# Eight 1 MB weight loads near the end of a two-layer trunk, each issued as five row pieces

## The chip, the cores and the metric

The kernel runs on one core of a Trainium2 chip. The metric is device time in microseconds (us), the median of several executions; lower is better. Names of engines are those of the profile: PE is TensorE, PEld its weight loads, DVE is VectorE, ACT is ScalarE, POOL is GpSimd and SP is SyncE, whose sequencer issues the weight loads. A DMA that SP issues is carried out by the core's 16 DMA engines.

## What is computed

Two layers of a hybrid encoder trunk over 256 tokens of width 1024. Each layer runs three branches (differential attention, a causal pooling mixer, attention to 256 memory tokens), gates and merges them, and then a channel mixer. In the second layer, where the change lies, the mixer is a top-2-of-8 expert SwiGLU:

```python
def moe_swiglu(h, w_router, w1, w3, w2):
    ...
    comb = jnp.einsum('tk,tke->te', gates, jax.nn.one_hot(idx, N_EXPERTS, dtype=h.dtype))
    out = jnp.zeros_like(ht)
    for e in range(N_EXPERTS):
        out = out + comb[:, e:e + 1] * swiglu(ht, w1[e], w3[e], w2[e])
    return out.reshape(B, S, D)
```

w1 and w3 of an expert are 1024 x 3584, w2 is 3584 x 1024, all float32.

## The kernel before

All weights lie in one DRAM tensor `w` of blocks of 128 rows x 2048 float32 (1 MB, 8 KB a row), laid out on the host in the order in which they are used. Half a block (128 x 1024) is a unit. The class `Stream` walks through the units: `load` (L190) takes a free 1 MB buffer, issues one block into it from SP (L201) and goes on as long as a buffer is free; `give` (L226) puts a buffer back after its last use and calls `load` again. The very first block and the very last one are cut into three column pieces (`ends`); all others are one DMA of 128 partitions x 8 KB.

The order of the blocks is fixed by `plan`. After the dense layer the expert stage goes through eight places of seven steps each; place 0 is expert 0, and the other experts are ranked at run time by their token counts, so that the block's address is a register on SP (`src`, `at`). A place has a fixed number of token rows, `ROWS = (96, 64, 96, 64, 96, 64, 96, 64)`. A step has an up part, `up` (L1179: four blocks, matmuls of 32 token columns against 256 weight columns in four array tiles), and a down part, `down` (L1205: two blocks), one step behind. So a place takes 42 blocks, and the last place, of 64 rows, takes the last 42 blocks of the run. After the last matmul the result is evacuated (L1224, L1226), scattered back to the tokens (L1128, L1133) and stored (`finish`, L853).

In the expert stage some eighteen buffers of 1 MB rotate: four of the ring, four that held split pairs before, and those of tiles that the attention no longer needs (`W.widen` calls). Matmuls here read the loaded float32 block directly, without a step in between (`raw`).

The framework gives every DMA one of a fixed set of semaphores, in turn; a DMA that takes a semaphore waits on SP until the DMA that had it before has landed. SP runs its program in order, so everything behind a waiting DMA waits too. A reader of a buffer waits for all DMAs that wrote it.

Of the kernel before, what the change touches and what calls it, by code (L numbers as in the profile page):

```python
# [32 lines left out]
ROWS = (96, 64, 96, 64, 96, 64, 96, 64)  # L33
LARGEST = [p for p in range(1, NE) if ROWS[p] == max(ROWS)]
RANKS = [0 if p == 0 else 1 + (LARGEST + [q for q in range(1, NE) if q not in LARGEST]).index(p) for p in range(NE)]
LANES = np.arange(512).reshape(4, 4, 32)


# [9 lines left out]
def plan():  # L48
# [21 lines left out]
    def lanes(e, parts):  # L70

        per = 512 // sum(len(p) for p in parts)
        units.extend([(t, e, np.arange(r + q, r + q + 128), p) for q in range(0, per * 128, 128)
                      for p in parts for t in ("moe_w1", "moe_w3")] for r in range(0, D, per * 128))
# [21 lines left out]
    for e in range(NE):  # L96
        for c in range(FE // 512):
            where["up", c] = len(units) // 2 - first - e * EXPERT
            if e == 0 and c == 0:
                lanes(e, [LANES[:, :2].transpose(1, 0, 2).ravel()])  # L100
                lanes(e, [LANES[j, 2:].ravel() for j in range(4)])
            else:
                lanes(e, [c * 512 + LANES[j].ravel() for j in range(4)])
            where["down", c] = len(units) // 2 - first - e * EXPERT
            units.extend([("moe_w2", e, c * 512 + LANES[:, q].ravel(), np.arange(D))] for q in range(4))
    order = [(0, k - first) for k in range(first)]
# [47 lines left out]
class Stream:  # L154
# [39 lines left out]
    def load(self, most=99):  # L194
        while self.loaded < self.total and self.free and most:
            slot = self.free.popleft()
            u, n = self.loaded, 2
            raw = slot[0]()
            ends = {0: (0, 512, 1024, 2048), self.total - 2: (0, 1024, 1536, 2048)}.get(u, (0, 2048))
            for c, e in zip(ends, ends[1:]):  # L200
                self.nc.sync.dma_start(raw[:, c:e], self.src(u, c, e - c))  # L201
            for i in range(n):
                self.raws[u + i] = (raw[:, i * 1024:(i + 1) * 1024], slot if i == n - 1 else None)
            self.loaded += n
            most -= 1
# [40 lines left out]
def trunk(ctx: ExitStack, tc: tile.TileContext, a, out, stage=99):  # L246
# [685 lines left out]
    for p in range(NE):  # L932
        nc.gpsimd.memset(ranks[:, p:p + 1], float(RANKS[p]))
        nc.gpsimd.memset(rows[:, p:p + 1], float(ROWS[p]))
# [449 lines left out]
```

## Time and profile before

| | before |
|---|---|
| median of 3 runs | 1632.04 us (1631.81 to 1632.33) |
| profiled execution | 1631.46 us, span 1629.7 us |
| PE busy | 1581.9 us, 97% |
| DVE / ACT busy | 645.4 us / 521.6 us |
| DMA moved | 493.78 MB, 303 GB/s over the span |
| 1 MB weight loads on SP | 455, median 19.8 us from issue to landing |

The span is the time from the first to the last instruction of one profiled execution; the device time of the same execution is a little longer. The page cuts the span into 40 slices of 40.7 us and gives the busy share of each engine and of the DMA engines in tenths. Below it stands the chain that ended last, and what each engine waited for. A busy PE is not a PE at its peak: matmul ends are modelled.

### The profile page before, as it was taken

The page shows a single profiled execution, that of the slowest core. Times are in us where ns is not written, and L with a number is a line of the kernel's source. Part 1 is how long each engine was busy: PE and PEld are TensorE (multiplying, and loading weights), DVE is VectorE, ACT ScalarE, POOL GpSimd, SP SyncE. Part 2 cuts the span into 40 slices and gives each one's busy share as a digit, 9 for nine tenths or more (in the row PEclk, how much of TensorE's full clock was granted, in tenths as well). Part 3 has the DMA queues.
Part 4 walks back from the last instruction along what each step waited for, and adds up shares of the span by engine and source line. Part 5 has one row for each costly group of instructions (what it writes and reads, how often), then busy time and mean ns, then how long its engine had stood idle before and what let it go on. Part 6 is the DMA issues. An engine that isn't in the chain of part 4 may idle for free.

```text
span 1629.7 us, 39421 instructions
## 1 busy us (share of the span) xinstructions
PE 1581.9 (97%) x17511; PEld 1110.2 (68%) x17511; DVE 645.4 (40%) x1261; ACT 521.6 (32%) x877; POOL 7.8 (0%) x36
## 2 busy tenths in 40 slices
PE   9999999999999999999999999999999998899987
PEld 6888788788888887787866555665556654466553
DVE  6676876655656666776410212112021120110201
ACT  7676654544545666554300101001000010000100
POOL 0000000000000000000000000000000000000000
PEclk9999999999999999999999999999999999999999
DMA  9544365454554434667889999999999999999996
GB/s 381 205 150 159 142 220 182 171 180 180 189 190 162 188 134 161 235 224 280 340 329 393 418 417 418 417 417 418 418 418 418 418 418 418 417 410 417 412 410 245
DMA packets 69809, 493.78 MB, mean 303 GB/s; under 512 B 7904, under 2 KB 8160, under 8 KB 10752
## 3 DMA queue, kind: packets, MB, share of 16 engines
q1 hardware_dynamic: 67824, 485.68, 75.4%
q0 software_dynamic: 1232, 4.82, 0.9%
q8 instruction: 139, 2.28, 0.6%
q10 hardware_dynamic: 576, 0.69, 0.1%
q14 instruction: 38, 0.31, 0.1%
HBM read 490.11 MB, written 1.05 MB: 301 GB/s over the span
## 4 chain that ended last, share of the span: by engine, by line
PE 76%; DMA 20%; DVE 1%; ACT 1%; issue 0%; SPq 0%; ACTq 0%
PE acc L392 41%; DMA raw<-in_w_dram 20%; PE acc L1179 18%; PE y L1205 9%; PE xgp L1042 1%; PE sc L1128 1%; PE ds L643 1%; PE tT L504 1%; PE do L683 1%; DMA E<-in_x_t_dram 0%; PE mo L587 0%; PE ms L554 0%; DVE pair L219 0%; DVE yf L1224 0%; ACT yf L1226 0%
## 5 line engine op out<-in xcount | busy, mean ns | idle before, releaser
L1179 PE MATMUL acc<-raw,xg 128*32 128x256 f32 (+1 forms) x8960 | 508.2, 378 | 19.6 <-DMA raw<-in_w_dram 17.9
L1179 PEld LDWEIGHTS acc<-raw,xg 128*32 128x32 f32 x8960 | 290.3, 110 | 216.8 <-issue 25.8
L219 DVE TENSOR_TENSOR pair<-raw,pair 128x1024 fp32r<-128x1024 f32 (+1 forms) x247 | 300.4, 1219 | 222.6 <-ACT pair L218 221.9
L392 PE MATMUL acc<-pair,bigB 128*128 128x512 f32 x1536 | 375.4, 399 | 2.2 <-ACT pair L218 1.7
L218 ACT ACTIVATE pair<-raw 128x1024 fp32r<-128x1024 f32 (+1 forms) x247 | 260.1, 1055 | 289.4 <-PE acc L392 275.7
L392 PEld LDWEIGHTS acc<-pair,bigB 128*128 128x128 f32 x1536 | 284.1, 188 | 72.0 <-ACT pair L218 2.6
L1205 PE MATMUL y<-raw,gt 128*32 128x256 f32 x4480 | 255.4, 379 | 9.0 <-DMA raw<-in_w_dram 8.0
L1190 DVE TENSOR_TENSOR junk<-acc,junk 128x256 f32<-128x256 f32 (+2 forms) x83 | 29.2, 377 | 562.0 <-ACT junk L1189 562.0
L1189 ACT ACTIVATE junk<-acc 128x256 f32<-128x256 f32 (+2 forms) x83 | 28.9, 348 | 664.4 <-PE acc L1179 663.1
L392 PE MATMUL acc<-pair,bigA 128*128 128x512 f32 (+1 forms) x960 | 219.8, 386 | 0.7 <-ACT g L822 0.4
L1205 PEld LDWEIGHTS y<-raw,gt 128*32 128x32 f32 x4480 | 147.5, 110 | 106.9 <-DMA raw<-in_w_dram 7.9
L392 PEld LDWEIGHTS acc<-pair,bigA 128*128 128x128 f32 x960 | 172.4, 188 | 38.9 <-ACT g L822 0.8
L392 PE MATMUL acc<-pair,E 128*128 128x512 f32 x456 | 108.8, 396 | 0.0
L392 PEld LDWEIGHTS acc<-pair,E 128*128 128x128 f32 x456 | 84.7, 188 | 20.9 <-issue 1.3
L1192 DVE STREAM_TRANSPOSE gt<-junk 128x128 f32<-128x128 f32 (+1 forms) x140 | 33.2, 283 | 1.0
L654 ACT ACTIVATE dp<-dp,dmn 128x128 f32<-128x128 f32 (+1 forms) x64 | 28.5, 446 | 10.1 <-DVE dmn L650 9.8
L1128 PE MATMUL sc<-ys,GT 96*128 96x512 f32 (+1 forms) x56 | 22.3, 477 | 9.1 <-ACT ys L366 8.3
L1133 DVE SCALAR_TENSOR_TENSOR total<-sc,misc,total 128x512 f32<-128x512 f32 x28 | 20.8, 750 | 24.8 <-PE sc L1128 24.6
L1226 ACT ACTIVATE yf<-y 32x256 f32<-32x256 f32 x48 | 18.0, 375 | 37.6 <-PE y L1205 37.1
L1042 PEld LDWEIGHTS xgp<-xg,x 128*128 128x128 f32 x160 | 20.8, 190 | 6.7 <-issue 6.6
L1224 DVE COPY yf<-y 32x256 f32<-32x256 f32 x32 | 13.4, 420 | 29.2 <-PE y L1205 28.9
L1049 ACT ACTIVATE xg<-xgp,cols 128x160 f32<-128x160 f32 (+2 forms) x20 | 6.0, 365 | 58.9 <-PE xgp L1042 58.9
(245 smaller groups left out, 783.5 us busy)
## 6 DMA issues: line engine op xcount, KB each, us to landing
raw<-in_w_dram SPq DMA_DIRECT2D x455, 1024.0 KB, 19.8
bb<-in_b_gate_dram POOLq DMA_DIRECT2D x6, 512.0 KB, 4.5
E<-in_mem_t_dram SPq DMA_DIRECT2D x2, 1024.0 KB, 10.8
raw<-in_w_dram SPq DMA_DIRECT2D x4, 256.0 KB, 10.0
raw<-in_w_dram SPq DMA_DIRECT2D x2, 512.0 KB, 12.6
x<-in_x_dram SPq DMA_DIRECT2D x1, 1024.0 KB, 13.5
E<-in_mem_dram SPq DMA_DIRECT2D x1, 1024.0 KB, 19.8
bias<-in_bias_dram POOLq DMA_DIRECT2D x1, 1024.0 KB, 8.0
```

Of the source, the lines that this page charges most:

```text
L218: nc.scalar.activation(t[:, 0, sl], src[:, sl], AF.Copy)
L219: nc.vector.tensor_tensor(t[:, 1, sl], src[:, sl], t[:, 0, sl].bitcast(F32), OP.subtract)
L392: nc.tensor.matmul(accs(tb, b)[:, :n], s, w[:, off:off + n], start=begin and (tb, b) not in started, stop=end and n_ == 2 and last[b] == ( ...
L654: nc.scalar.activation(p[:, 1, m, :kl], p[:, 0, m, :kl], AF.Exp, scale=-1.0, bias=mn[:, m:m + 1], accum_out=s0[:, b, h + i:h + i + 1] if m ...
L1042: nc.tensor.matmul(t[:, i], x[:, tb, (k0 + i) * 128:(k0 + i + 1) * 128], G[tuple(es)][:, tb], start=tb == 0, stop=tb == 1)
L1128: nc.tensor.matmul(t, gt[:, tb], ys[p][:, j * 512:(j + 1) * 512], start=p == 0, stop=p == len(ys) - 1)
L1133: nc.vector.scalar_tensor_tensor(xo, t, comb[:, tb, e:e + 1], x[:, tb, sl] if e == 0 else xo, op0=OP.mult, op1=OP.add)
L1179: nc.tensor.matmul(t[32 * j:32 * j + 32, c0:c0 + n], XG[e][:, k, 32 * r:32 * r + 32], w[:, (4 * m + j) * n:(4 * m + j + 1) * n], start=k = ...
L1189: nc.scalar.activation(g[:, r0:r1], v[:, :, 0], AF.Silu)
L1190: nc.vector.tensor_tensor(g[:, r0:r1], v[:, :, 1], g[:, r0:r1], OP.mult)
L1192: nc.vector.transpose(gts[i][:, r, 4 - width // 32:].rearrange("p q t -> p (q t)"), g[:, r])
L1205: nc.tensor.matmul(t[32 * j:32 * j + 32, c0:c0 + 256], gt[:, r, q], w[:, 256 * j:256 * j + 256], start=first and q == 0 and r < 2, stop=la ...
```

## The change

`load` issues eight of the blocks, those 24 to 17 from the end, as five DMAs instead of one: rows 0 to 95, then rows 96 to 103, 104 to 111, 112 to 119 and 120 to 127, each of 8 KB a row. The bytes, the buffer and the readers are the same.

```diff
+LEAN = range(-24, -16)
...
             ends = {0: (0, 512, 1024, 2048), self.total - 2: (0, 1024, 1536, 2048)}.get(u, (0, 2048))
+            cuts = [0, 128]
+            if u // 2 - self.total // 2 in LEAN:
+                cuts = [0, 96, 104, 112, 120, 128]
             for c, e in zip(ends, ends[1:]):
-                self.nc.sync.dma_start(raw[:, c:e], self.src(u, c, e - c))
+                src = self.src(u, c, e - c)
+                for p, q in zip(cuts, cuts[1:]):
+                    self.nc.sync.dma_start(raw[p:q, c:e], src[p:q])
```

## Rows read from the trace of the kernel before

**Rows 1.** The page: busy tenths of PE and DMA, and GB/s, in 40 slices.

```profile
PE   9999999999999999999999999999999998899987
...
DMA  9544365454554434667889999999999999999996
GB/s 381 205 150 159 142 220 182 171 180 180 189 190 162 188 134 161 235 224 280 340 329 393 418 417 418 417 417 418 418 418 418 418 418 418 417 410 417 412 410 245
```

**Rows 2.** Chain that ended last, 1480 to 1632 us: start us, us, what.

```profile
1488.01 4.87 PE acc L1179 x89
1492.88 21.24 DMA raw<-in_w_dram
...
1514.24 19.88 DMA raw<-in_w_dram
...
1615.44 3.69 PE y L1205 x64
```

**Rows 3.** What SP's queue waited for, 1490 to 1630 us: us in total, times, longest.

```profile
SPq L201 <- DMA raw<-in_w_dram: 89.6, 45, 2.8
...
SPq L201 <- PE acc L1179: 1.0, 3, 0.4
SPq L201 <- PE y L1205: 0.8, 2, 0.4
```

**Rows 4.** Timeline of SP, two stretches: start us, us, instruction, count.

```profile
1539.18 64.00 SPq L201 DMA_DIRECT2D raw<-in_w_dram  x26
...
1557.13 0.33 SPq L201 DMA_DIRECT2D raw<-in_w_dram  x1
```

**Rows 5.** Line L201, 1480 to 1630 us: ns min/median/max of each instruction; landing.

```profile
L201 SPq MOVE raw<-in_w_dram x49: 29/29/29, 1480.4 to 1600.8; - x49
L201 SPq DMA_DIRECT2D raw<-in_w_dram x49: 332/333/338, 1480.4 to 1602.8; - x49
L201 SPq FUSED_REGOPS  x48: 55/55/75, 1480.8 to 1600.7; - x48
L201 SPq EVENT_SEMAPHORE  x47: 17/17/17, 1480.3 to 1597.9; - x47
...
DMA to landing us min/median/max: 15.1/20.1/21.3
```

**Rows 6.** The DMA view, 1300 to 1500 us: packets of all sizes; SP's queue with packets, MB, share.

```profile
DMA packets 11405, 83.26 MB, mean 416 GB/s; under 512 B 1267, under 2 KB 1267, under 8 KB 1267
...
q1 hardware_dynamic: 11376, 82.82, 100.4%
```

**Rows 7.** Windows of 2 us at the end; the last two columns are DMA share, GB/s.

```profile
1602.00:1604.00 2.00, 1.54 (x32) 0.70 (x28) 0.00 (x0) 0.00 (x0) 0.00 (x0) 1.00 0.86 340
1604.00:1606.00 2.00, 1.43 (x28) 0.65 (x24) 0.00 (x0) 0.00 (x0) 0.00 (x0) 1.00 0.68 266
1606.00:1608.00 2.00, 1.44 (x30) 0.66 (x24) 0.00 (x0) 0.00 (x0) 0.00 (x0) 1.00 0.53 209
1608.00:1610.00 2.00, 1.80 (x32) 0.80 (x27) 0.00 (x0) 0.14 (x1) 0.00 (x0) 1.00 0.48 201
1610.00:1612.00 2.00, 1.55 (x31) 1.13 (x32) 0.93 (x3) 0.25 (x1) 0.00 (x0) 1.00 0.51 213
1612.00:1614.00 2.00, 1.53 (x32) 0.73 (x28) 0.00 (x0) 0.00 (x0) 0.00 (x0) 1.00 0.50 209
1614.00:1616.00 2.00, 1.34 (x28) 0.68 (x24) 0.00 (x0) 0.00 (x0) 0.00 (x0) 1.00 0.48 189
1616.00:1618.00 2.00, 2.00 (x44) 1.48 (x39) 0.00 (x0) 0.00 (x0) 0.00 (x0) 1.00 0.26 89
```

**Rows 8.** Chain that ended last, in an earlier place of 64 rows.

```profile
1335.68 6.91 PE acc L1179 x128
```

**Rows 9.** DMA issues of the whole run: KB each, median us to landing.

```profile
out_dram<-total SPq DMA_DIRECT2D x2, 256.0 KB, 2.9
...
E<-in_x_t_dram SPq DMA_DIRECT2D x1, 128.0 KB, 3.2
```

## The prediction, made before the changed kernel ran

> **What bounds the kernel.** I began with the page's slices [rows 1]. From the 23rd slice on the DMA rate is flat at about 417 GB/s with a busy share of 9 tenths or more, while PE's own digits fall in the last slices: the expert stage streams weights at a ceiling. Then the chain of waits [rows 2]: PE is on it until 1493 us, and from there to 1615 us, where PE takes over again, it is almost nothing but weight loads, one hanging on another, each some 20 us long; PE adds its last 3.7 us and the scatter. In a place of 64 rows PE needs 6.91 us for four blocks, 1.73 us a block [rows 8]; a block arrives every 2.5 us. So in the last place the time is set by when the last block has landed, and the changed loads lie in the middle of that stretch: the 26 issues from 1539.2 us on [rows 4] are 23 whole blocks and the three pieces of the last, so the first of them is the block 24 from the end, and the one 17 from the end goes out at 1557.1 us. A microsecond lost or won by the loads there reaches the end unless it is made up later, and nothing in the last 60 us has room to make it up.
>
> Next, how the loads are paced. One block takes 1048576 bytes / 418 GB/s = 2.51 us [rows 1]; it lands 20.1 us after its issue [rows 5]. 20.1 / 2.51 = 8: eight DMAs are outstanding, always. The chain shows the same: a load is issued 0.12 us after an earlier one landed (1492.88 + 21.24 = 1514.12, the next at 1514.24) [rows 2]. And SP waited 45 times in this stretch for a weight DMA and five times, 1.8 us in all, for a buffer [rows 3]. So the limit is eight DMAs in flight, counted in DMAs and not in bytes.
>
> Last, the end of the stream [rows 7]. The busy share does not drop from 1 to 0: it falls between 1602 and 1606 us to 0.5, stays there with 200 to 213 GB/s, and goes to 0 after 1617 us. Half of the 16 engines had finished, and the other half still worked at the same rate each (209 / 8 = 26.1 GB/s, as 418 / 16). The share missing from 1602 to 1616 us is 2.96 windows of 2 us, 5.9 us of all engines or 11.8 us of eight. So one half of the engines, the leading half, runs 11.8 us ahead of the other, the lagging half. Which numbers they have no view shows.
>
> **The change, step by step.** *Rows per engine.* 82.82 MB are 79 blocks, and they go with 11376 packets, 144 a block; 1267 packets, 16 a block, are under 512 B [rows 6]. So 128 remain: one packet per row of 8 KB. At 26.1 GB/s a row takes 0.314 us. The piece of 96 rows gives each engine 6 rows. A piece of 8 rows is 8 packets, so it cannot be on more than eight engines; I take it that the four pieces of a block go to the same eight. These carry 6 + 4 = 10 rows a block (3.13 us), the other eight 6 (1.88 us), where all carried 8 (2.51 us). Over eight blocks that is 16 rows, 5.0 us, moved from one half to the other.
>
> [...]
>
> *SP's queue.* Five DMAs a block cost SP 5 x (0.333 + 0.029 + 0.055 + 0.017 us) = 2.2 us [rows 5], below 3.13 us, so the issuing itself is hidden by the transfers. What isn't hidden is the limit of eight. From 1539.2 to 1557.1 us eight old blocks land on the lagging half, and each landing lets SP issue one DMA. Before, that was eight blocks; now it is 96, 8, 8, 8, 8, 96, 8 and 8 rows, not two blocks. If the pieces go to the leading half, it had 20.1 - 11.8 = 8.3 us of old work and gets 6 + 4 + 6 + 2 = 18 rows, 5.6 us: it runs dry and its lead is spent on waiting. The lagging half ends its old work at 1557.0 us and then has two pieces of 6 rows.
>
> *From there on.* Still to be moved by the eight engines: 2 rows of the second block and six blocks of 10, 62 rows. The first of them waits for the first large piece, which lands on the lagging half at 1557.0 + 1.9 = 1558.9 us. From issue to landing without data I take 2.6 us: a store of 256 KB takes 2.9 us, less 0.6 of data, and a load of 128 KB 3.2 us, less 0.3 [rows 9]. So the first row lands at 1559.0 + 2.6 + 0.3 = 1561.9 us, the other 61 follow in 19.1 us, and 0.3 us go between the first few, whose issues come singly: 1581.3 us. Sixteen whole blocks at 2.51 us follow on the same engines: 1621.5 us. The same count for the kernel before is 1557.0 + 24 x 2.51 = 1617.2 us, and its transfers do stop there [rows 7]. Difference: +4.3 us. With the fixed part at 2.3 or 2.9 us it is +4.0 or +4.6; if the restart cost nothing, +1.7.
>
> If the eight are the lagging half, nothing runs dry: the half that ends last carries 16 rows more, +5.0 us. I sum with +4.3: the two differ by less than the uncertainty.
>
> *What costs nothing.* 32 more DMAs with their small packets: 8 rows alone are 2.51 us and so is a block, so a small packet is under 0.01 us. Matmuls that read a split block wait for five semaphores: at SP's 17 ns a wait that is 0.6 us for all eight blocks, covered by PE's 0.78 us of slack in every block; uncovered, it would be those 0.6 us. Buffers: eighteen stand against eight loads in flight, and the waits for them are 1.8 us [rows 3].
>
> Sum: 1631.46 us (the profiled execution) + 4.3 = 1635.8; the median stands 0.58 us above that execution: **1636.3 us**.
>
> **Rivals.** *The rows shift and nothing runs dry: faster.* Half the engines stand idle for the last 11.8 us. If the pieces go to the leading half and SP gets them out without the wait for the eighth DMA back, so that the leading half always has rows, it ends 5.0 us later and the lagging half 5.0 us earlier, with 1.8 us of lag left: 1632.04 - 5.0 = 1627.0 us. For it: the 0.5 share [rows 7], and that 5.0 us is near half of 11.8. Against it: the 45 waits [rows 3]. It decides if the leading half's queue outlasts the 18 us from 1539 us on; by the rows it holds 13.9 us of work.
>
> *Rows that share a way into the buffer: slower still.* [...] If neighbours share a path, a row takes longer: between 0.31 us (no sharing) and 2.51 us (all eight share one). With a threefold time, near the middle on a doubling scale, four pieces cost 4 x 0.63 = 2.5 us more a block; over the 6.2 blocks of the 62 rows that is 15.6 us: 1652 us. Twofold it is +7.8 (1644), fourfold +23 (1660). Nothing in this trace is so narrow, so nothing speaks for or against it.
>
> [...]
>
> *The pieces don't lean on one half.* If successive pieces go to different eights in turn, every engine still carries 8 rows a block, the lag stays, and the end moves by less than the restart cost: 1632 to 1634 us. That a piece is at most eight packets leaves open which eight engines take them.
>
> **Chances.** Forecast (same eight, no sharing) 0.40; sharing 0.27; faster 0.17; no lean 0.16. A measurement of this kernel can tell about 0.2%, 3.3 us, from no change. The forecast's low end, +1.7, lies under that, so I give 0.08 of its 0.40 to "same". Slower by over 0.2%: 0.32 + 0.27 = 0.59; within: 0.16 + 0.08 = 0.24; faster: 0.17. The range takes in the forecast's bounds, the no-lean case, the half of the faster case that falls short of its full gain, and sharing up to about threefold: 1629 to 1654 us; what it leaves out (full gain 0.09, more sharing 0.08) is under 0.2.
>
> **What would show it.** In the profile after, 447 loads of 1024 KB, 8 of 768 KB and 32 of 64 KB; packets under 512 B are 32 x 8 = 256 more than before if each small piece uses eight engines, and twice that if it uses sixteen. Windows of 2 us: from about 1547 to 1560 us the DMA share falls towards 0.5 to 0.7, then stays near 0.8 (16 engines carry 128 rows in the time of 10 on eight) until about 1581 us; the last 12 us no longer stand at 0.5 if the leading half was the one loaded, and stand there longer if the other was. SP's waits for a weight DMA rise from 45 to about 75. With sharing, the middle stretch has a share near 1 (packets take longer) at 200 to 300 GB/s and lasts over 30 us. The forecast is wrong if the rate stays near 418 GB/s through 1540 to 1580 us, or if the end comes before 1630 us.

## The result, and the profile after

The changed kernel takes 1655.12 us (1654.03 to 1656.54) against 1631.92 in the same comparison: a ratio of 1.0143, 95% interval 1.0131 to 1.0155. It is 23 us slower. The forecast was slower by 4.3 us, with a range that ends at 1654.

The page of the changed kernel, first the DMA slices and then packets, SP's queue and SP's larger pieces:

```profile
span 1652.3 us, 39533 instructions
...
DMA  9544455455554544658989999999999999999897
GB/s 380 202 146 158 152 202 186 176 181 181 192 185 167 178 145 159 258 203 313 350 336 397 418 417 418 417 417 418 418 418 417 418 418 419 417 411 413 263 281 306
DMA packets 70067, 493.79 MB, mean 299 GB/s; under 512 B 8161, under 2 KB 8417, under 8 KB 11009
...
q1 hardware_dynamic: 68080, 485.69, 75.5%
...
raw<-in_w_dram SPq DMA_DIRECT2D x447, 1024.0 KB
raw<-in_w_dram SPq DMA_DIRECT2D x8, 768.0 KB
```

The stream is as before up to the 37th slice [rows 1 have 417, 412, 410 and 245 in the last four]; then two slices fall to 263 and 281 GB/s. SP's queue has 68080 packets. The page of the kernel before has 67824:

```profile
q1 hardware_dynamic: 67824, 485.68, 75.4%
```

So 256 came with the 32 small pieces: eight each, where a whole block has 16. That fits eight engines a piece, half of those at work on whole blocks (a share of 1.01), and loads of eight neighbouring rows by themselves kept a share of 0.50, eight of 16, in the second run of dead loads below.

What the stretch looks like, in windows of 10 us and as a whole (the last two columns are DMA share and GB/s):

```profile
1540.00:1550.00 10.00, 10.00 (x165) 5.45 (x168) 2.85 (x6) 0.38 (x1) 0.00 (x0) 1.00 0.88 250
1550.00:1560.00 10.00, 9.25 (x175) 5.27 (x167) 0.93 (x3) 0.38 (x1) 0.00 (x0) 1.00 0.66 201
1560.00:1570.00 10.00, 5.54 (x96) 3.01 (x88) 0.00 (x0) 0.00 (x0) 0.00 (x0) 1.00 0.63 166
...
1590.00:1600.00 10.00, 5.94 (x64) 3.80 (x64) 0.00 (x0) 0.00 (x0) 0.00 (x0) 0.66 0.89 243
...
1540.00:1600.00 60.00, 41.52 (x613) 22.78 (x612) 4.71 (x12) 1.15 (x3) 0.00 (x0) 0.89 0.80 219
```

The same 60 us of the kernel before:

```profile
1540.00:1600.00 60.00, 53.36 (x906) 29.30 (x902) 6.57 (x18) 1.92 (x5) 0.00 (x0) 0.99 1.01 413
```

This closes the account. In these 60 us 219 GB/s move 13.14 MB, which at 418 GB/s would take 31.4 us; 28.6 us are lost. The share says in which way. At 0.80 the engines stood idle for 20% of the time, 12.0 us. While they were busy they were slow: a row of 8 KB took on average 0.80 x 16 x 8192 B / 219 GB/s = 0.48 us of one engine, where whole blocks had shown 0.314, and that is the other 16.6 us. Two things are set against the 28.6: 0.7 us that the kernel before loses in the same window (413 instead of 418), and the tail. Windows of 2 us at the end of the changed kernel:

```profile
1636.00:1638.00 2.00, 1.47 (x28) 0.64 (x20) 0.00 (x0) 0.00 (x0) 0.00 (x0) 1.00 0.99 389
1638.00:1640.00 2.00, 1.87 (x36) 1.43 (x40) 0.00 (x0) 0.00 (x0) 0.00 (x0) 1.00 0.39 143
```

Where the kernel before worked its last 12 us with half its engines [rows 7], all sixteen now end within a microsecond or two. The 5.9 us that half the engines had stood idle are won back. 28.6 - 0.7 - 5.9 = 22.0 us, and the spans differ by 22.6.

The chain of waits shows that not only the new pieces are slow:

```profile
1516.88 20.37 DMA raw<-in_w_dram
...
1537.36 26.53 DMA raw<-in_w_dram
...
1618.19 19.81 DMA raw<-in_w_dram
```

The block issued at 1537.36 us is a whole one, the last before the split ones. It took 26.5 us to land, with cut blocks beside it, against about 20 for whole blocks before and after the stretch.

### The profile page after: what moved, and what is told of

Read it like the earlier page. It is cut to its first block, busy times and chain, and to the rows that moved or that the text cites. A ratio compares the mean times of both kernels' runs of the same rounds, so it can differ in the third digit from the quotient of the medians.

```text
span 1652.3 us, 39533 instructions
## 1 busy us (share of the span) xinstructions
PE 1589.7 (96%) x17511; PEld 1111.7 (67%) x17511; DVE 645.5 (39%) x1261; ACT 521.7 (32%) x877; POOL 7.9 (0%) x36
## 3 DMA queue, kind: packets, MB, share of 16 engines
q1 hardware_dynamic: 68080, 485.69, 75.5%
q8 instruction: 139, 2.28, 0.6%
## 4 chain that ended last, share of the span: by engine, by line
PE 77%; DMA 20%; DVE 1%; ACT 1%; issue 0%; SPq 0%; ACTq 0%
PE acc L398 41%; DMA raw<-in_w_dram 19%; PE acc L1185 19%; PE y L1211 9%; PE xgp L1048 1%; PE sc L1134 1%; PE ds L649 1%; PE tT L510 1%; PE do L689 1%; DMA E<-in_x_t_dram 0%; PE mo L593 0%; PE ms L560 0%; DVE pair L225 0%; DVE yf L1230 0%; PE xT L445 0%
## 5 line engine op out<-in xcount | busy, mean ns | idle before, releaser
L1134 PEld LDWEIGHTS sc<-ys,GT 96*128 96x128 f32 (+1 forms) x56 | 9.5, 200 | 22.7 <-ACT ys L372 11.5
```

Of the source, the lines that this page charges most:

```text
L1134: nc.tensor.matmul(t, gt[:, tb], ys[p][:, j * 512:(j + 1) * 512], start=p == 0, stop=p == len(ys) - 1)
```

## The experiments

Three theories stood: the small pieces' neighbouring rows slow each other (A); the queue of eight DMAs and the uneven rows alone cost the 23 us (B); every DMA over a part of the rows is slow, the 96-row piece too (C). Four kernels came first.

**The small pieces take every fourth row.**

```diff
-                for p, q in zip(cuts, cuts[1:]):
-                    self.nc.sync.dma_start(raw[p:q, c:e], src[p:q])
+                rows = [slice(p, q) for p, q in zip(cuts, cuts[1:])]
+                if len(cuts) > 2:
+                    rows = [slice(0, 96)] + [slice(96 + j, 128, 4) for j in range(4)]
+                for r in rows:
+                    self.nc.sync.dma_start(raw[r, c:e], src[r])
```

> Same eight blocks, same count of DMAs and same rows per engine as the changed kernel, but each 8-row piece takes every fourth row of rows 96 to 127 instead of eight neighbours. Theory A (the small pieces' neighbouring rows slow each other): the time falls to the sum without sharing, about 1632 + 4 = 1636 us. Theory B (the queue of eight DMAs and the uneven rows alone cost the 23 us): no change, 1655 us. Theory C (the 96-row piece is slowed too, on all engines): it stays over 1645 us.

Measured: 1650.9 us, ratio 1.0115 (1.0098 to 1.0132), 4 us less than the change. SP's issues in this kernel (min/median/max in ns, then a stretch of the timeline), and below them those of the changed kernel:

```profile
L210 SPq DMA_DIRECT2D raw<-in_w_dram x51: 326/644/825, 1535.7 to 1602.7; - x51
...
1565.70 28.05 SPq L210 DMA_DIRECT2D raw<-in_w_dram  x33
...
L207 SPq DMA_DIRECT2D raw<-in_w_dram x81: 277/332/364, 1481.1 to 1625.5; - x81
```

The 4 us are not the price of the neighbourhood. A piece of every fourth row takes SP about 0.64 us to issue, where one of eight neighbours takes 0.28, and SP gets out 33 DMAs in 28.05 us, 0.85 us each or 4.25 us a block. Five issues one right behind the other take 4.07 us (1566.61 to 1570.68), so nearly all of that is SP's own time. At that pace the stretch is slow whatever its rows cost, and this run cannot tell what the neighbourhood is worth. Theory A falls with the next run.

**Two pieces, 96 and 32 rows.** No small pieces and no uneven engines: SP's queue has 67952 packets, 128 more than before, 16 for each piece of 32 rows.

```diff
-                cuts = [0, 96, 104, 112, 120, 128]
+                cuts = [0, 96, 128]
```

> The eight blocks in two DMAs, of 96 and 32 neighbouring rows; if 32 rows spread over all 16 engines, each engine carries 8 rows a block as before. Theory C (a piece of fewer than 128 rows is slow because its rows collide): +10 to +17 us, 1642 to 1649. Theory A (only the 8-row pieces) and B: 0 to +1 us, 1632 to 1633.

Measured: 1654.98 us, ratio 1.0143 (1.0127 to 1.0160), the same as the change itself. Cutting a block once between two rows costs as much as the whole change, so A alone is out. The window of this kernel, and one of its tail:

```profile
1540.00:1600.00 60.00, 41.73 (x630) 23.77 (x625) 4.71 (x12) 1.15 (x3) 0.00 (x0) 0.91 0.95 239
...
1634.00:1636.00 2.00, 1.54 (x32) 0.80 (x28) 0.11 (x1) 0.00 (x0) 0.00 (x0) 1.00 0.52 214
```

Here the engines are hardly idle (0.95) and a row takes 0.95 x 16 x 8192 / 239 GB/s = 0.52 us. The tail at half share is still there. So the two kernels come to the same time by different sums: the change idles 9 us more and has rows that are a little faster, and it wins the tail back.

**Five pieces by columns.** The same sizes and count, each over all 128 rows.

```diff
-                cuts = [0, 96, 104, 112, 120, 128]
+                ends = (0, 1536, 1664, 1792, 1920, 2048)
```

> The same eight blocks in five DMAs of the same sizes (768 KB and four times 64 KB), but cut by columns, each over all 128 rows: same count in the queue of eight, no uneven engines, no neighbours. Theory A and C (sharing): 0 to +3 us, 1632 to 1635. Theory B (the count in the queue): most of the 23 us stays, over 1645 us.

Measured: 1640.13 us, ratio 1.0052 (1.0036 to 1.0069): 8 us slower, between the two expectations. SP's timeline in the middle of it:

```profile
1559.70 23.46 SPq L207 DMA_DIRECT2D raw<-in_w_dram  x33
```

SP gets out 33 pieces in 23.46 us, 0.71 us each, so a block of five takes 3.6 us and not 2.51. I had put SP's own time at 2.2 us a block; one right behind the other the pieces go out 0.54 to 0.60 us apart, 2.8 us a block. The stretch as a whole, and the end of the stream:

```profile
1540.00:1590.00 50.00, 40.14 (x676) 22.54 (x672) 5.25 (x15) 1.54 (x4) 0.00 (x0) 1.00 0.84 296
...
1622.00:1624.00 2.00, 1.33 (x28) 0.59 (x21) 0.00 (x0) 0.00 (x0) 0.00 (x0) 1.00 0.99 383
1624.00:1626.00 2.00, 2.00 (x44) 1.47 (x40) 0.00 (x0) 0.00 (x0) 0.00 (x0) 1.00 0.23 80
```

At 296 GB/s the 50 us lose 14.6. Of these 8.0 are idle engines (0.84), and 6.6 are busy ones that are slower with the narrow pieces among their work: on average 0.84 x 16 x 8192 / 296 = 0.37 us for 8 KB. The tail at half share is gone here too, although a piece does not lean on few engines: SP's queue has 72432 packets, 4608 more than before, 144 for each of the 32 added pieces, as many as a whole block has. 14.6 - 0.7 - 5.9 = 8.0 us, and the spans differ by 8.2.

**Two odd blocks.** An attempt to lean on few engines with two DMAs instead of five.

```diff
-LEAN = range(-24, -16)
+LEAN = (-24, -20)
...
-                cuts = [0, 96, 104, 112, 120, 128]
+                cuts = [0, 119, 128]
```

> Leans on few engines with two DMAs instead of five: only blocks 24 and 20 from the end, cut in 119 and 9 rows. If 119 rows go on seven engines (17 rows each) and 9 on nine, the leading half takes about 20 rows more (6.3 us) and the lagging half 14 to 16 rows less (4.4 us). Without slow rows in the piece: 1632 - 4.5 = 1627.5 us. If its neighbouring rows slow each other about as in the changed kernel (a row in 0.55 instead of 0.31 us): 34 rows take 18.7 us, beyond the leading half's lead, and the time is 1632 to 1641 us.

Measured: 1653.64 us, ratio 1.0133 (1.0116 to 1.0150). Two cut blocks cost 22 us, more than either expectation. SP's queue has 67824 packets, as before, so the two pieces of a block have 16 small packets together; that agrees with seven engines and nine, if each adds one, and no view shows which engines they are. SP's timeline from 1539 to 1545 us:

```profile
1539.13 2.66 SPq L207 DMA_DIRECT2D raw<-in_w_dram  x2
```

A window right after, and one near the end:

```profile
1545.00:1550.00 5.00, 5.00 (x99) 2.99 (x92) 0.78 (x3) 0.00 (x0) 0.00 (x0) 1.00 0.97 205
...
1630.00:1635.00 5.00, 3.87 (x64) 2.06 (x64) 0.93 (x3) 0.38 (x1) 0.00 (x0) 1.00 0.19 75
```

From 1545 to 1550 us the only cut block issued is the one of 1539.13 us; all others in flight are whole. Yet the share is 0.97 and the rate 205 GB/s: on average the engines take 0.62 us a row (0.97 x 16 x 8192 / 205). Eight engines at 26.1 GB/s would move 209 GB/s by themselves. So unless more than eight engines were held up by their own rows of the cut block, engines that were writing whole blocks were slowed by it. At the end the share of 0.19 for some 10 us says that about three engines were left with a backlog. The 60 us from 1540 us on:

```profile
1540.00:1600.00 60.00, 38.24 (x584) 22.20 (x579) 4.25 (x12) 1.15 (x3) 0.00 (x0) 0.83 0.96 277
```

They lose 20.2 us, 2.4 to idle engines and 17.8 to slow rows; the tail costs some 2 us more than before. So slow rows are most of the 22 us.

The next three asked whether the cut between rows is what matters, whether the place does, and what the engines do when nothing else runs.

**Two pieces by columns.**

```diff
-                cuts = [0, 96, 104, 112, 120, 128]
+                ends = (0, 1536, 2048)
```

> The eight blocks in two DMAs as in the run with 96 and 32 rows, of the same sizes (768 and 256 KB), but cut by columns, each over all 128 rows. Sharing (a DMA over part of the rows makes engines collide): no collisions here, 0 to +2 us, 1632 to 1634. If two DMAs a block instead of one were what costs 23 us (queue of eight, issue): 1655.

Measured: 1631.85 us, ratio 1.0001 (0.9992 to 1.0011). The same bytes in the same two sizes as the cut between rows 95 and 96, and the time does not change. The stretch, and the window in which its tail begins:

```profile
1540.00:1600.00 60.00, 51.67 (x892) 28.34 (x884) 5.92 (x18) 1.92 (x5) 0.00 (x0) 1.00 0.97 379
...
1612.00:1614.00 2.00, 1.52 (x32) 0.72 (x27) 0.00 (x0) 0.00 (x0) 0.00 (x0) 1.00 0.73 294
```

The stretch isn't free: at 379 GB/s it loses 4.9 us more than before. The tail at half share, 12 us long before, is down to some 5 us and gives about as much back. But 239 GB/s with a cut between rows stands against 379 with a cut between columns. C holds, against B.

**The eight blocks earlier.**

```diff
-LEAN = range(-24, -16)
+LEAN = range(-84, -76)
```

> The changed kernel with its eight blocks moved to 84 to 77 from the end, the first eight blocks of the place before, which has 96 rows and where PE works almost without a gap on blocks that landed earlier. If the loads' lost time is what counts and buffers ahead of PE can hide part of it: +10 to +20 us, 1642 to 1652. If nothing is ahead: +23, 1655. If all of it is hidden by PE's own pace and regained: under +3.

Measured: 1655.41 us, ratio 1.0146 (1.0129 to 1.0163). I had thought that part of the loss could be hidden in a place where PE works on blocks that landed earlier. Nothing is: from 1450 us on the stream is back at 418 GB/s and runs without a gap to the end, and what it lost before it has lost.

**Dead loads on idle engines.** The kernel before, with 32 loads put behind its last store in the program, four of a kind, each waiting for the one before it. One run. The output is not touched.

```diff
     finish((nc.sync, nc.scalar), total[0])
+    pr, ps = raw_slot("raw0")(), W.at(0, 0)
+    for _ in range(4):
+        nc.sync.dma_start(pr[:128], ps[:128])
+    for _ in range(4):
+        nc.sync.dma_start(pr[:8], ps[:8])
...
```

> The kernel before with 32 dead loads on idle DMA engines after the last store, four of a kind, each over the rows of the one before it: 128 rows; 8 neighbouring rows; 8 rows at every fourth partition; 8 at every eighth; 16, 64, 96 and 32 neighbouring rows; always from the first rows of the same block, 8 KB a row. What is told apart is the step from one to the next of a kind. [...]

SP's timeline, in the order in which the kinds stand in the expectation (start, us, count; one step is the length less 0.33 us, through three):

```profile
1625.95 7.52 SPq L1365 DMA_DIRECT2D raw<-in_w_dram  x2
1637.94 8.01 SPq L1367 DMA_DIRECT2D raw<-in_w_dram  x4
1648.16 7.58 SPq L1369 DMA_DIRECT2D raw<-in_w_dram  x4
1657.48 8.11 SPq L1371 DMA_DIRECT2D raw<-in_w_dram  x4
1667.43 8.37 SPq L1373 DMA_DIRECT2D raw<-in_w_dram  x4
1678.19 14.50 SPq L1375 DMA_DIRECT2D raw<-in_w_dram  x4
1696.97 16.12 SPq L1377 DMA_DIRECT2D raw<-in_w_dram  x4
1717.97 9.55 SPq L1379 DMA_DIRECT2D raw<-in_w_dram  x4
```

The last load of 128 rows is issued at 1633.13 and lands for the issue at 1637.94 us: 4.8 us. It is the only clean step of its kind, since the first two loads went out before the last stores (1612.40 and 1620.43 us) and the third beside them. 96 rows take 5.26 us, 64 take 4.72, 32 take 3.07, 16 take 2.68. What the engines did in the steps of 128, 64 and 96 rows:

```profile
1633.13:1637.94 4.81, 0.00 (x0) 0.00 (x0) 0.00 (x0) 0.00 (x0) 0.00 (x0) 0.50 0.61 218
1678.19:1696.97 18.78, 0.00 (x0) 0.00 (x0) 0.00 (x0) 0.00 (x0) 0.00 (x0) 0.50 0.47 112
1696.97:1717.97 21.00, 0.00 (x0) 0.00 (x0) 0.00 (x0) 0.00 (x0) 0.00 (x0) 0.50 0.56 150
```

By share and rate a row takes 0.61 x 16 x 8192 / 218 = 0.37 us in the load of 128 rows, 0.55 in those of 64 and 0.49 in those of 96. So three quarters of a block take at least as long as the whole, and half of it about as long, with nothing else running.

The steps of the three kinds of 8 rows differ by at most 0.2 us (2.56, 2.42, 2.59). They are not a clean comparison: the issue itself, which is part of a step, takes SP 0.28 us for neighbours, but 0.64 for every fourth partition and 0.57 for every eighth. From the end of the issue the neighbours are the slowest, 2.28 us against 1.78 and 2.02. The engines' time a row is about 0.4 us in all three (shares of 0.08, 0.09 and 0.08 at 26, 28 and 26 GB/s). So a single load of neighbours does not show a fourfold price; whether it shows a smaller one is open.

That left open where rows meet: at the source in DRAM or at the destination.

**Dead loads of 8 rows, up to eight in flight.** Again behind the last store of the kernel before; always the same source rows, into eight buffers, sixteen of a kind. One run.

```diff
+    for i in range(16):
+        nc.sync.dma_start(prs[i % 8][:8], ps[:8])
+    for i in range(16):
+        nc.sync.dma_start(prs[i % 8][0:32:4], ps[:8])
+    for i in range(16):
+        nc.sync.dma_start(prs[i % 8][0:64:8], ps[:8])
+    for i in range(16):
+        nc.sync.dma_start(prs[i % 8][:8], ps[:8])
```

> The kernel before with 64 dead loads of 8 rows after the last store, sixteen of a kind into eight different buffers, so that up to eight are in flight at once; always the same source rows. Kinds: 8 neighbouring partitions, every fourth, every eighth, neighbours again. [...] If the DRAM side or the piece as such is slow, the three kinds take the same time.

Windows in the second, third and fourth kind (the columns after the length are clock, DMA share and GB/s):

```profile
1645.00:1650.00 5.00, 0.50 0.33 95
...
1655.00:1660.00 5.00, 0.50 0.40 105
...
1670.00:1675.00 5.00, 0.50 0.50 52
```

With eight neighbouring partitions the share is 0.50, eight engines busy all the time, and they move 52 GB/s together: 0.50 x 16 x 8192 / 52 = 1.26 us a row, four times 0.314. The same source rows into every fourth or every eighth partition move at 95 and 105 GB/s. So it is the neighbourhood at the destination that holds them at 52, not the source as such. What holds the other two near 100 GB/s is SP. Its issues by kind (every fourth, every eighth, neighbours again; ns min/median/max), the third kind in the timeline, and the waits of the second and the last kind:

```profile
L1367 SPq DMA_DIRECT2D raw<-in_w_dram x16: 623/624/781, 1636.1 to 1648.8; - x16
L1369 SPq DMA_DIRECT2D raw<-in_w_dram x16: 563/564/591, 1649.5 to 1658.7; - x16
L1371 SPq DMA_DIRECT2D raw<-in_w_dram x16: 271/272/463, 1659.3 to 1671.8; - x16
1649.49 9.72 SPq L1369 DMA_DIRECT2D raw<-in_w_dram  x16
...
SPq L1371 <- DMA raw<-in_w_dram: 7.7, 9, 0.9
SPq L1367 <- DMA raw<-in_w_dram: 4.1, 7, 1.4
```

An issue to partitions four or eight apart takes SP 0.62 or 0.56 us, one to neighbours 0.27. The loads of the third kind go out 0.61 us apart without a wait, 107 GB/s; those of the second, once the waits for the first kind are over, 0.67 us apart, 98 GB/s. Only the neighbours are held by their landing. So SP sets the pace of every fourth and of every eighth, and the run does not tell the two apart.

That neighbours at the destination are what slows the cut blocks in the stream is argued from the two runs of dead loads: 1.26 us a row for eight neighbours, and 4.72 us for 64 rows, near the 4.81 of a whole block. No run separates source and destination in the stream itself.

**Two halves of 64 rows.**

```diff
-                cuts = [0, 96, 104, 112, 120, 128]
+                cuts = [0, 64, 128]
```

> The eight blocks in two pieces of 64 rows each: every engine carries 4 + 4 rows. On idle engines 64 rows took 4.72 us from one to the next, as long as 128 rows (4.81), so a half piece moves at half the rate. If that holds in the stream, a block takes up to 5 us instead of 2.51: +10 to +20 us, 1642 to 1652. If it is only DMAs of 96 rows that are slow: 0 to +2.

Measured: 1656.4 us, ratio 1.0149 (1.0132 to 1.0166), a little over the upper end. It is not a matter of the number 96.

**Three pieces by columns.**

```diff
-                cuts = [0, 96, 104, 112, 120, 128]
+                ends = (0, 1536, 1792, 2048)
```

> The eight blocks in three column pieces (768 KB, 128 and 128 KB), all over 128 rows. The five column pieces cost 8 us. If that is the queue of eight DMAs holding too few bytes, three pieces cost a part of it, +2 to +5 us. If it is SP's issue time alone (about 0.55 us a DMA: five take 2.8 us, longer than the 2.51 us of a block, three take 1.7 us), it costs nothing: 1632 us within 1.

Measured: 1633.03 us, ratio 1.0008 (0.9998 to 1.0018). That is 1.2 us, not clear of nothing. The total speaks for SP's time per DMA, and against a starved queue, as the reason why five pieces cost 8. But the total hides what the stretch loses:

```profile
1540.00:1600.00 60.00, 53.34 (x902) 29.32 (x906) 7.54 (x20) 1.92 (x5) 0.00 (x0) 0.98 0.95 370
```

At 370 GB/s it loses 6.2 us more than before, and the shorter tail gives most of it back. Part of the loss is idle engines (0.95), part slower narrow pieces, as with five. What share of the idle time is SP's and what the queue's stays open.

No version here beats the kernel before. What would (moving rows to the leading half without cutting a block between rows) was not found.

## Why the prediction was wrong

The sign, the stretch and the bottleneck were right: the stream is the critical path, and what it loses reaches the end, except for what the leading half's lead of 11.8 us pays. So, as far as the packets show it, was the number of engines of a small piece: 256 more for 32 pieces, eight each. Which half they belong to is not shown. I had taken the end of the tail as the sign of the leading half, but the tail is gone in the kernel with five column pieces too, and these lean on neither half (144 packets a piece, as a whole block).

That engines would run dry was right as well, and about in its size. A net loss of 4.3 us, with 5.9 us of idle tail won back, meant some 10 us of idle engines; the share of 0.80 over 60 us says 12.0.

The step that failed is the price of a row. "At 26.1 GB/s a row takes 0.314 us" was read from whole blocks and applied to pieces. In the stretch a row took 0.48 us on average. For the 62 rows of the sum that alone is, as an estimate, 62 x (0.48 - 0.314) = 10 us. Besides, I let the whole blocks still in flight land on time, at 1557.0 us; slowed by the pieces beside them, the last one landed at 1563.9 (the chain's 26.53 us), 6.9 us later. 4.3 + 10 + 7 = 21 us; the measured difference is 23. The stream was back at full rate at about 1600 us, not at 1581.

The rival with shared paths, with chance 0.27, was the nearest, but drawn too narrowly. I let only the 8-row pieces share, and took a threefold time. The kernel with 96 and 32 rows shows the large piece to be slow as well, and the chain's 26.53 us shows a whole block slowed beside the pieces. Its threefold price, 1652 us, came within about 3 us of the result, and that is luck: it charged 32 small pieces for what a cut between rows costs without any small piece (1654.98 us). The fourfold price, 1660 us, is 5 us off. A fourfold time did come out for eight neighbours on idle engines (1.26 us a row), but the mean row in the stream took 0.48. That neighbours share a path stays a supposition: the runs show the slower rows, not what they share. The range ended at 1654, 1 us short.

The faster rival fell with the same step: its price assumed 0.314 us a row as well. Of what I said would show, the numbers of loads and packets and the share falling to 0.63 came out. Of the signs of sharing the low rate came (166 to 250 GB/s for some 60 us), the share near 1 only with 96 and 32 rows (0.95). SP's waits for a weight DMA did not rise to 75, they are 47:

```profile
SPq L207 <- DMA raw<-in_w_dram: 94.7, 47, 3.8
```

So of the 77 issues in this time at least 30 waited for no load. That fits small pieces that had landed before their turn came; the trace does not name the loads.

## What to carry to other kernels

A load of all 128 rows should not be cut between rows where the stream is the bound: here that costs some 3 us a block even in two pieces, and it slows the whole loads beside it. Cut it by columns if it must be cut; two pieces cost no time here, where half the engines had 12 us of lead to give up, and five cost 8 us. A total that does not move can hide a loss that such a lead pays for: look at the stretch. And a price per row or per byte taken from whole loads holds for whole loads (here 0.314 us a row, against 0.48 in the stretch with cut blocks); for a narrower shape that the trace does not have, measure a few dead loads behind the last store first, several at a time.

## What the runs showed that I had not expected

96 rows alone on idle engines take no less than 128 (5.26 us against one clean step of 4.8). A cut load in flight slows whole loads: one landed in 26.5 us instead of 20. Eight neighbouring partitions take 52 GB/s with up to eight loads in flight, but one such load alone shows no fourfold price. A load to partitions four or eight apart takes SP 0.62 or 0.56 us to issue, one to neighbours 0.27. And moving the eight blocks 60 blocks forward changed nothing (1655.41 us), although PE had work there.
